# Moving one gate step in the projection phase, and splitting the last norm of a two-layer hybrid decoder trunk

## The chip, the cores and the metric

The kernel runs on one core of one Trainium2 chip. The metric is the device time of one execution in microseconds (us). An execution under the hardware profiler gives the rows shown below; the plain executions give the median.

## What is computed

Two layers, each of two sublayers with a LayerNorm behind each. 256 tokens, model width 1024, everything float32:

```python
for l in range(2):
    proj = x @ w_in[l]            # rnn input, GeLU gate, q / kv latents, rotary key, gates A and B
    y_rnn = gelu(g_rnn) * rg_lru(causal_dwconv(x_rnn), gx_w, ga_w, ...)   # gate_x, gate_a: 16 blocks of 64
    y_mla = mla_attention(q_lat, kv_lat, k_rope, ...)                     # 16 heads, causal
    mix = (sigmoid(gate_a) * y_rnn + sigmoid(gate_b) * y_mla) @ w_out
    x = layer_norm(ALPHA * x + mix, ln1_g, ln1_b)
    ffn = (gelu(conv3(x @ w_up)[gate]) * conv3(x @ w_up)[val]) @ w_down   # d_ff 3072
    x = layer_norm(ALPHA * x + ffn, ln2_g, ln2_b)
```

## The kernel before

**Precision.** Each float32 operand is split into a rounded part (hi) and a rest (lo): ScalarE (ACT) writes hi with a copy, VectorE (DVE) writes lo with a subtraction. A product is then three matmuls, hi·hi, hi·lo and lo·hi (`mm3`, lines 191 to 193). Weights come from HBM by DMAs of the SP queue into four buffers `raw`, and `load_split` (lines 182 and 183) splits each key in two halves of 1024 columns into the tiles `wh` and `wl`, which have six buffers each, so three keys at a time. A buffer comes free when the last matmul that reads it is done.

**Tiling.** Tokens are two tiles of 128 rows (`t` = 0, 1), channels are chunks of 128. `proj_pair` makes one projection of 256 channels for all 256 tokens: 2 halves (m) x 8 chunks x 3 = 48 matmuls of 256 columns into one bank of PSUM, each half of the bank by 24 of them. The first half of the weights is read last by the 36th matmul, the second by the 48th.

**The order.** TensorE (PE) runs in the order in which the program issues; the other engines are put in order by a planner (a list scheduler with its own simulated times) within what the dependences and `behind` allow. For the mixer sublayer the issue order is the string `ORDER`, a list of steps run once per layer. The steps that matter here:

- `x0` to `x3` (`conv_branch`): one projection each, then per chunk of 128 channels a convolution: ACT line 598, three DVE steps on line 601, then the split of the result into `xch` (ACT, line 607) and `xcl` (DVE, line 608).
- `P` with a digit (`fetch`): load and split of one key of the list `FETCH`: `P6` the recurrent gates' weights, `P8` and `P9` and `Pa` the gate-A keys 1, 2 and 3, `Pb`, `Pc`, `Pd` the gate-B keys 0, 1 and 2.
- `e0` to `e3` (`gates`, line 611): for two chunks each, 6 matmuls per chunk on `xch`, `xcl` and the weights of `P6`, then two sigmoids on ACT (line 619) per chunk. `e3` works on chunks 6 and 7, the output of `x3`.
- `a0` to `a3` (`gate_branch`): one projection with a gate-A key, one sigmoid on ACT (line 626), one product on DVE (line 628).
- `N` (`rnn_gates`): DVE and ACT work on all gates, with four long activations of each kind. `act_step` keeps the sigmoids and the activations of `N` in program order on ACT.

In each layer PE therefore runs ... a1, e2, e3, a2, a3, h1 (a gate-B projection) ... and the six buffers of `wh` hold, at that time, the weights of `P6` until `e3` has read them.

**The end.** `finish` (line 357) runs the last accumulation of a down (or output) projection: it completes tile 0, issues the norm of tile 0, then the last five chunks of tile 1 (for `h` = 0, then for `h` = 1, 512 columns and one PSUM bank each, 15 matmuls per `h`), then the norm of tile 1. `LayerNorm.tile` (line 389) does, per half of 512 columns, the residual add out of PSUM (line 397) and the statistics (line 401), then the aggregate (402), 403, the power on GpSimd (404), and for the very last norm lines 408 and 411 for each half and one DMA of 256 KB for each half from the SP queue (line 413).

**The start.** Lines 202 to 206 issue `WARM` = 8 float32 matmuls of zeros (two passes each in the profile) ahead of the first real matmul, while the first transfers arrive.

Of the kernel before, what the change touches and what calls it, by code (L numbers as in the profile page):

```python
# [11 lines left out]
F32 = mybir.dt.float32  # L12
# [3 lines left out]
ALU = mybir.AluOpType  # L16

P = 128
D = 1024
S = 256  # L20
NT = S // P
# [21 lines left out]
ORDER = (  # L43
# [5 lines left out]
)  # L49
HELD = 4  # L50
WARM = 8
KORD = (0, 1, 4, 5, 2, 3, 6, 7)
NPAIR = DFF // P
ALPHA = (2 * DEPTH) ** 0.25
# [69 lines left out]
def trunk(ctx, tc, x_tok, x_chan, pos, wts, par, lnrow, consts, out):  # L124
    nc = tc.nc
    A = nc.scalar
    V = nc.vector
# [6 lines left out]
    sm = ctx.enter_context(tc.tile_pool(name="sm", bufs=2))  # L134
# [5 lines left out]
    def bank(name):  # L140
        return pp.tile([P, 512], F32, tag="pb", name=name)
# [48 lines left out]
    def mm3(o, lh, ll, rh, rl, start, stop):  # L190
        T.matmul(o, lhsT=lh, rhs=rh, start=start, stop=False)  # L191
        T.matmul(o, lhsT=lh, rhs=rl, start=False, stop=False)  # L192
        T.matmul(o, lhsT=ll, rhs=rh, start=False, stop=stop)  # L193
# [10 lines left out]
    spare = bank("spare")  # L204
    for _ in range(WARM):
        T.matmul(spare[:, :P], lhsT=idle, rhs=idle, start=True, stop=True)
# [23 lines left out]
    for i in range(1, 4):  # L230
# [9 lines left out]
        out=mask[:, P:], in_=mask[:, P:], pattern=[[-1, P]],  # L240
# [106 lines left out]
        return hi[:, o + a:o + b], lo[:, o + a:o + b]  # L347

    def out_last(accs, t, n, wts_of, act_of, hc):
        for h, c in hc:  # L350
            hi, lo = wts_of(c)
            ah, al = act_of(c)
            mm3(accs[t][h], ah[:, t * P:(t + 1) * P], al[:, t * P:(t + 1) * P],
                hi[:, 512 * h:512 * h + 512], lo[:, 512 * h:512 * h + 512],
                False, c == n - 1)

    def finish(ln, accs, n, wts_of, act_of, late):
        out_last(accs, 0, n, wts_of, act_of, [(h, n - 1) for h in range(2)])
        ln.tile(0, accs)
        hc = [(h, c) for h in range(2) for c in range(n - late, n)]  # L360
        out_last(accs, 1, n, wts_of, act_of, hc[:-HELD])
        if not ln.last:
            ln.turn(0)
        out_last(accs, 1, n, wts_of, act_of, hc[-HELD:])
        ln.tile(1, accs)
# [9 lines left out]
    class LayerNorm:  # L375
# [13 lines left out]
        def tile(self, t, accs):  # L389
            l, last = self.l, self.last  # L390
            z = big.tile([P, D], F32, tag="xres", name="z", bufs=4)
            st = sm.tile([P, 2, 6], F32, tag="st", name="st")
            mv = sm.tile([P, 2], F32, tag="mv", name="mv")
            rs = sm.tile([P, 1], F32, tag="rs", name="rs")
            hs = [slice(512 * h, 512 * h + 512) for h in range(2)]
            for h in range(2):
                V.scalar_tensor_tensor(
                    out=z[:, hs[h]], in0=self.xres[t][:, hs[h]], scalar=ALPHA, in1=accs[t][h],
                    op0=ALU.mult, op1=ALU.add,
                )  # L400
                V.bn_stats(st[:, h], z[:, hs[h]])
            V.bn_aggr(mv, st.rearrange("p a b -> p (a b)"))
            V.tensor_scalar(out=rs, in0=mv[:, 1:2], scalar1=EPS, scalar2=None, op0=ALU.add)
            G.tensor_tensor(out=rs, in0=rs, in1=nhalf[:, 0:1], op=ALU.pow)
            g, b = self.gb
            if last:
                for h in range(2):
                    V.scalar_tensor_tensor(out=z[:, hs[h]], in0=z[:, hs[h]], scalar=mv[:, 0:1],
                                           in1=g[:, hs[h]], op0=ALU.subtract, op1=ALU.mult)
                for h in range(2):  # L410
                    V.scalar_tensor_tensor(out=z[:, hs[h]], in0=z[:, hs[h]], scalar=rs,
                                           in1=b[:, hs[h]], op0=ALU.mult, op1=ALU.add)
                    nc.sync.dma_start(out=out[t * P:(t + 1) * P, hs[h]], in_=z[:, hs[h]])
                return
            nmr = sm.tile([P, 1], F32, tag="nmr", name="nmr")
            V.scalar_tensor_tensor(out=nmr, in0=mv[:, 0:1], scalar=-1.0, in1=rs,
                                   op0=ALU.mult, op1=ALU.mult)
            for c in (0, 256):
                V.tensor_scalar(out=z[:, c:c + 256], in0=z[:, c:c + 256], scalar1=mv[:, 0:1],
                                scalar2=rs, op0=ALU.subtract, op1=ALU.mult)  # L420
            A.activation(z[:, hs[1]], z[:, hs[1]], AF.Identity, scale=rs, bias=nmr)
            self.res.append(z)
# [85 lines left out]
    for l in range(DEPTH):  # L508
# [335 lines left out]
        later[0] = False  # L844
        ln = LayerNorm(l, 0, xres, False)
        finish(ln, oacc, 8, lambda c: ow[c], mer_of, 5)
        tp = [bank("upt") for _ in range(NB)]

# [84 lines left out]
        for j in range(NPAIR - LAG, NPAIR - 1):  # L933
            out_chunk(dacc, j, dw[j], hq[j], (0, 1) if j < NPAIR - LATE else (0,))
        ln = LayerNorm(l, 1, xres, l == DEPTH - 1)
        finish(ln, dacc, NPAIR, lambda c: dw[c], lambda c: hq[c], LATE)
        if l < DEPTH - 1:
            xs, xres = ln.xs, ln.res
# [119 lines left out]
```

## Time and profile before

| | us |
|---|---|
| median of 3 runs | 804.9 (804.83 to 805.35) |
| the profiled execution, its own time | 804.24 |
| its span, first to last instruction | 802.4 |
| PE busy in the span | 791.0 |
| DVE, ACT busy | 650.5, 509.1 |
| granted TensorE clock, mean | 0.997 |

The profiled execution is 0.66 us below the median. PE is busy nearly all the time, so what remains to be read is where it is not: 802.4 - 791.0 = 11.4 us, of which the last 7.4 us lie behind its last matmul.

### The profile page before, as it was taken

What the parts mean: (1) busy time and instruction counts of PE and PEld (TensorE: products, weight loads), DVE (VectorE), ACT (ScalarE), POOL (GpSimd) and SP (SyncE); (2) the same over time, 40 slices, a digit from 0 to 9 for tenths busy, and PEclk for the clock granted to TensorE, in tenths of its full rate; (3) what the DMA queues carried; (4) which work ended last, traced back from release to release, by engine and by line L of the source; (5) the groups of instructions that cost most, each with busy time, mean ns of one, the idle gap of its engine ahead of it and who ended that gap; (6) DMA issues with size and microseconds to landing.
All of it is one profiled execution on the core that took longest, in us unless ns stands there. A gap on an engine that the chain in (4) does not pass through costs nothing.

```text
span 802.4 us, 14518 instructions
## 1 busy us (share of the span) xinstructions
PE 791.0 (99%) x5712; PEld 741.2 (92%) x5712; DVE 650.5 (81%) x1260; ACT 509.1 (63%) x910; POOL 10.9 (1%) x27
## 2 busy tenths in 40 slices
PE   9999999999999999999999999999999999999996
PEld 8999899878999999999899999998799999999994
DVE  6998889997699977667777886999887998677755
ACT  5765987783777465556475579688567665555540
POOL 1000000000000000000000000000000000000000
PEclk9999999999999999999999999999999999999998
DMA  8955436524356655435625544563524756655311
GB/s 313 344 185 211 152 115 242 187 85 181 158 210 263 210 177 209 174 122 218 236 79 201 183 169 139 173 219 121 208 76 184 276 196 211 210 165 203 106 53 53
DMA packets 26468, 144.76 MB, mean 180 GB/s; under 512 B 3360, under 2 KB 7072, under 8 KB 11808
## 3 DMA queue, kind: packets, MB, share of 16 engines
q1 hardware_dynamic: 26400, 143.84, 50.6%
q8 instruction: 45, 0.74, 0.4%
q14 instruction: 23, 0.19, 0.1%
HBM read 140.68 MB, written 1.05 MB: 177 GB/s over the span
## 4 chain that ended last, share of the span: by engine, by line
PE 97%; DMA 1%; DVE 1%; ACT 1%; SPq 0%; issue 0%; DVEq 0%
PE proj L193 18%; PE proj L191 18%; PE proj L192 18%; PE dacc L191 6%; PE dacc L192 6%; PE dacc L193 6%; PE oacc L191 2%; PE oacc L192 2%; PE oacc L193 2%; PE sps L756 2%; PE yps L797 2%; PE ptp L783 1%; PE latp L192 1%; PE latp L193 1%; PE latp L191 1%; PE sps L754 1%
## 5 line engine op out<-in xcount | busy, mean ns | idle before, releaser
L193 PE MATMUL proj<-xhi,wl 128*128 128x256 f32 x1216 | 344.2, 283 | 0.1
L191 PE MATMUL proj<-xhi,wh 128*128 128x256 f32 x1216 | 344.1, 283 | 0.0
L192 PE MATMUL proj<-xlo,wh 128*128 128x256 f32 x1216 | 343.6, 283 | 0.0
L183 DVE TENSOR_TENSOR wl<-raw,wh 128x1024 fp32r<-128x1024 f32 (+5 forms) x226 | 241.9, 1089 | 50.4 <-ACT wh L182 49.9
L182 ACT ACTIVATE wh<-raw 128x1024 fp32r<-128x1024 f32 (+5 forms) x226 | 208.7, 952 | 103.0 <-PE proj L192 88.4
L192 PEld LDWEIGHTS proj<-xlo,wh 128*128 128x128 f32 x1216 | 232.9, 192 | 1.7
L191 PEld LDWEIGHTS proj<-xhi,wh 128*128 128x128 f32 x1216 | 232.9, 192 | 1.6
L193 PEld LDWEIGHTS proj<-xhi,wl 128*128 128x128 f32 x1216 | 232.9, 192 | 0.7 <-DVE wl L183 0.7
L899 DVE SCALAR_TENSOR_TENSOR u<-proj,par,u 128x255 f32<-128x255 f32 (+1 forms) x176 | 83.5, 479 | 39.2 <-ACT u L896 37.1
L896 ACT ACTIVATE u<-proj,par 128x256 f32<-128x256 f32 x88 | 49.1, 558 | 94.0 <-DVE u L899 71.5
L191 PE MATMUL dacc<-wsh,hh 128*128 128x512 f32 x192 | 76.2, 397 | 0.0
L192 PE MATMUL dacc<-wsl,hh 128*128 128x512 f32 x192 | 75.9, 395 | 0.0
L193 PE MATMUL dacc<-wsh,hl 128*128 128x512 f32 x192 | 75.9, 395 | 0.0
L183 DVE TENSOR_TENSOR wsl<-raw,wsh 128x1024 fp32r<-128x1024 f32 (+2 forms) x66 | 69.8, 1077 | 0.0
L182 ACT ACTIVATE wsh<-raw 128x1024 fp32r<-128x1024 f32 (+2 forms) x66 | 59.7, 937 | 0.0
L193 PEld LDWEIGHTS dacc<-wsh,hl 128*128 128x128 f32 x192 | 36.1, 188 | 8.9
L191 PEld LDWEIGHTS dacc<-wsh,hh 128*128 128x128 f32 x192 | 36.2, 189 | 7.0
L192 PEld LDWEIGHTS dacc<-wsl,hh 128*128 128x128 f32 x192 | 36.1, 188 | 6.9
L196 ACT ACTIVATE hh<-u 128x256 fp32r<-128x256 f32 x48 | 19.6, 408 | 13.7 <-DVE u L907 13.7
L191 PE MATMUL oacc<-wh,mhi 128*128 128x512 f32 x64 | 26.6, 415 | 0.0
L192 PE MATMUL oacc<-wl,mhi 128*128 128x512 f32 x64 | 25.0, 391 | 0.0
L193 PE MATMUL oacc<-wh,mlo 128*128 128x512 f32 x64 | 25.0, 391 | 0.0
(213 smaller groups left out, 1132.2 us busy)
## 6 DMA issues: line engine op xcount, KB each, us to landing
raw<-in_wts SPq DMA_DIRECT2D x114, 1024.0 KB, 4.9
raw<-in_wts SPq DMA_DIRECT2D x8, 832.0 KB, 4.9
gb<-in_lnrow SPq DMA_DIRECT2D x8, 512.0 KB, 8.0
raw<-in_wts SPq DMA_DIRECT2D x4, 672.0 KB, 4.1
raw<-in_wts SPq DMA_DIRECT2D x7, 336.0 KB, 6.6
raw<-in_wts SPq DMA_DIRECT2D x4, 512.0 KB, 4.5
xres<-in_x_tok SPq DMA_DIRECT2D x2, 512.0 KB, 6.0
k<-krot SPq DMA_DIRECT2D x8, 128.0 KB, 2.4
```

Of the source, the lines that this page charges most:

```text
L182: behind(A.activation(h, w, AF.Copy), after[0])
L183: lo_ins = V.tensor_tensor(out=lo[:, c - a:d - a], in0=w, in1=h.bitcast(F32), op=ALU.subtract)
L191: T.matmul(o, lhsT=lh, rhs=rh, start=start, stop=False)
L192: T.matmul(o, lhsT=lh, rhs=rl, start=False, stop=False)
L193: T.matmul(o, lhsT=ll, rhs=rh, start=False, stop=stop)
L196: A.activation(hi, src, AF.Copy)
L754: T.matmul(sps[:, :P], lhsT=q96[:, h4, :P], rhs=k96[:, h4, :P], start=True, stop=True)
L756: T.matmul(sps[:, P:P + S], lhsT=q96[:, h4, P:], rhs=k96[:, h4], start=True, stop=True)
L783: T.transpose(ptp[:, b * P:(b + 1) * P], sns[hh][:, b * P:(b + 1) * P], ident)
L797: T.matmul(yps[hh * 64:hh * 64 + 64, t * P:S], lhsT=vs[:, hv:hv + 64], rhs=pts[hh][:, 2 * t * P:(2 + t) * P], start=t == 0, stop=t == 1)
L896: ea = A.activation(dst, src, AF.Identity, scale=pcol(l, "fw", 96 + ch), bias=pcol(l, "fb", ch))
L899: ev = V.scalar_tensor_tensor(out=dst[:, k:], in0=src[:, :S - k], scalar=pcol(l, "fw", 48 * (2 - k) + ch), in1=dst[:, k:], op0=ALU.mult, o ...
```

## The change

Three edits. In `ORDER` the step `e3` goes behind `a2` and `Pc`, in both layers. `WARM` goes from 8 to 7. In the last norm, the accumulation of tile 1's second half of 512 columns is issued as two parts of 256 columns (all five chunks for the first part, then all for the second), its residual add and statistics are done in four pieces of 256 columns, and the rows of both token tiles are written in three pieces of 512, 256 and 256 columns, the middle one from the ACT queue.

```diff
-    "e3 a2 Pc N a3 h1 R0 Pd h2 h0 b0+ w0 R1 p0 Pe h3 q0 b1+ r0 L1+ b2 k0 v01 p1 r1 s0 q1 "
+    "a2 Pc e3 N a3 h1 R0 Pd h2 h0 b0+ w0 R1 p0 Pe h3 q0 b1+ r0 L1+ b2 k0 v01 p1 r1 s0 q1 "
-WARM = 8
+WARM = 7
@@ out_last
-        for h, c in hc:
-            hi, lo = wts_of(c)
+        for h, c, *cols in hc:
+            a, b = cols or (0, 512)
+            hi, lo = (w[:, 512 * h + a:512 * h + b] for w in wts_of(c))
             ah, al = act_of(c)
-            mm3(accs[t][h], ah[:, t * P:(t + 1) * P], al[:, t * P:(t + 1) * P],
-                hi[:, 512 * h:512 * h + 512], lo[:, 512 * h:512 * h + 512],
-                False, c == n - 1)
+            mm3(accs[t][h][:, a:b], ah[:, t * P:(t + 1) * P], al[:, t * P:(t + 1) * P],
+                hi, lo, False, c == n - 1 and b == 512)
@@ finish
-        hc = [(h, c) for h in range(2) for c in range(n - late, n)]
+        if ln.last:
+            hc = [(h, c, a, a + w) for h, a, w in ((0, 0, 512), (1, 0, 256), (1, 256, 256))
+                  for c in range(n - late, n)]
+        else:
+            hc = [(h, c) for h in range(2) for c in range(n - late, n)]
@@ LayerNorm.tile
-            for h in range(2):
+            w = 256 if last and t == NT - 1 else 512
+            n = D // w
+            for h in range(n):
+                cs = slice(w * h, w * h + w)
+                acc_h = accs[t][w * h // 512][:, w * h % 512:w * h % 512 + w]
                 V.scalar_tensor_tensor(
-                    out=z[:, hs[h]], in0=self.xres[t][:, hs[h]], scalar=ALPHA, in1=accs[t][h],
+                    out=z[:, cs], in0=self.xres[t][:, cs], scalar=ALPHA, in1=acc_h,
                     op0=ALU.mult, op1=ALU.add,
                 )
-                V.bn_stats(st[:, h], z[:, hs[h]])
-            V.bn_aggr(mv, st.rearrange("p a b -> p (a b)"))
+                V.bn_stats(st[:, h], z[:, cs])
+            V.bn_aggr(mv, st[:, :n].rearrange("p a b -> p (a b)"))
@@ LayerNorm.tile, last norm
-                for h in range(2):
-                    V.scalar_tensor_tensor(out=z[:, hs[h]], in0=z[:, hs[h]], scalar=rs,
-                                           in1=b[:, hs[h]], op0=ALU.mult, op1=ALU.add)
-                    nc.sync.dma_start(out=out[t * P:(t + 1) * P, hs[h]], in_=z[:, hs[h]])
+                for i, (c, d) in enumerate(((0, 512), (512, 768), (768, 1024))):
+                    V.scalar_tensor_tensor(out=z[:, c:d], in0=z[:, c:d], scalar=rs,
+                                           in1=b[:, c:d], op0=ALU.mult, op1=ALU.add)
+                    dma = nc.scalar if i == 1 else nc.sync
+                    dma.dma_start(out=out[t * P:(t + 1) * P, c:d], in_=z[:, c:d])
```

## Rows read from the trace of the kernel before

**Rows 1.** Page, part 1: busy us (share of span) and instructions.
```profile
PE 791.0 (99%) x5712; PEld 741.2 (92%) x5712; DVE 650.5 (81%) x1260; ACT 509.1 (63%) x910; POOL 10.9 (1%) x27
```

**Rows 2.** Waits of PE, whole span: waiter, awaited, total us, times, longest.
```profile
PE gates L192 <- DVE xcl L608: 1.0, 1, 1.0
PE gates L191 <- ACT xch L607: 0.8, 1, 0.8
PE latp L191 <- ACT wh L182: 0.6, 2, 0.3
```

**Rows 3.** Timeline of PE, layer 0: start, us, instruction, [idle before <-releaser].
```profile
85.62 0.28 PE L193 MATMUL gates<-xch,wl 128*128 128x256 f32 x1
86.71 0.38 PE L191 MATMUL gates<-xch,wh 128*128 128x256 f32 x1 [0.82 <-ACT xch L607]
88.09 0.38 PE L192 MATMUL gates<-xcl,wh 128*128 128x256 f32 x1 [0.99 <-DVE xcl L608]
...
88.78 0.29 PE L191 MATMUL proj<-xhi,wh 128*128 128x256 f32 x1
```

**Rows 4.** Timeline of ACT, the same stretch.
```profile
85.24 1.12 ACT L182 ACTIVATE wh<-raw 128x1024 fp32r<-128x1024 f32 x1
86.19 0.47 ACT L607 ACTIVATE xch<-xc 128x256 fp32r<-128x256 f32 x1
...
90.06 2.13 ACT L182 ACTIVATE wh<-raw 128x1024 fp32r<-128x1024 f32 x2
...
93.19 1.06 ACT L182 ACTIVATE wh<-raw 128x1024 fp32r<-128x1024 f32 x1 [0.28 <-PE proj L192]
94.62 1.06 ACT L182 ACTIVATE wh<-raw 128x1024 fp32r<-128x1024 f32 x1 [0.38 <-PE proj L192]
```

**Rows 5.** Timeline of DVE, the same stretch.
```profile
87.61 0.42 DVE L608 TENSOR_TENSOR xcl<-xc,xch 128x256 fp32r<-128x256 f32 x1
...
91.27 2.36 DVE L183 TENSOR_TENSOR wl<-raw,wh 128x1024 fp32r<-128x1024 f32 x2 [0.59 <-ACT wh L182]
```

**Rows 6.** Timelines of DVE and PE, the same place in layer 1.
```profile
480.22 0.42 DVE L608 TENSOR_TENSOR xcl<-xc,xch 128x256 fp32r<-128x256 f32 x1
...
481.47 0.28 PE L191 MATMUL gates<-xch,wh 128*128 128x256 f32 x1
```

**Rows 7.** Timeline of all engines, the end.
```profile
794.17 0.39 PE L192 MATMUL dacc<-wsl,hh 128*128 128x512 f32 x1
...
794.40 0.40 PE L193 MATMUL dacc<-wsh,hl 128*128 128x512 f32 x1
794.84 0.69 DVE L397 SCALAR_TENSOR_TENSOR z<-z,dacc 128x512 f32<-128x512 f32 x1 [0.83 <-PE dacc L193]
795.56 0.69 DVE L401 BATCH_NORM_STATS2 st<-z 128x6 f32<-128x512 f32 x1
...
797.92 1.41 DVE L411 SCALAR_TENSOR_TENSOR z<-z,rs,gb 128x512 f32<-128x512 f32 x2
```

**Rows 8.** Timeline of DVE, two independent 256-column steps back to back.
```profile
617.47 0.47 DVE L899 SCALAR_TENSOR_TENSOR u<-proj,par,u 128x255 f32<-128x255 f32 x1
...
617.86 0.47 DVE L899 SCALAR_TENSOR_TENSOR u<-upf,par,u 128x254 f32<-128x254 f32 x1
```

**Rows 9.** Timelines of PE and ACT: a half bank is read after a projection.
```profile
760.64 0.28 PE L193 MATMUL proj<-xhi,wl 128*128 128x256 f32 x1
...
760.96 0.56 ACT L896 ACTIVATE u<-proj,par 128x256 f32<-128x256 f32 x1 [2.32 <-PE proj L193]
```

**Rows 10.** Windows at the end: us, busy by engine, clock, DMA share, GB/s.
```profile
799.60:800.20 0.60, 0.00 (x0) 0.00 (x0) 0.00 (x0) 0.00 (x0) 0.00 (x0) 0.50 1.02 379
800.20:800.60 0.40, 0.00 (x0) 0.00 (x0) 0.00 (x0) 0.00 (x0) 0.00 (x0) 0.50 1.06 394
```

**Rows 11.** Timeline of PE and ACT, the start.
```profile
1.05 3.78 PE L206 MATMUL spare<-idle 128*128 128x128 f32 x16 [1.05 <-DVE lruw L334]
...
9.52 1.76 ACT L182 ACTIVATE wh<-raw 128x336 fp32r<-128x336 f32 x4 [0.23 <-DMA raw<-in_wts]
```

More of the change, by code (lines that the diff above doesn't have):

```diff
@@ L391, in tile @@
             z = big.tile([P, D], F32, tag="xres", name="z", bufs=4)
-            st = sm.tile([P, 2, 6], F32, tag="st", name="st")
+            st = sm.tile([P, 4, 6], F32, tag="st", name="st")
             mv = sm.tile([P, 2], F32, tag="mv", name="mv")
```

## The prediction

> **What bounds the kernel now.** I read the page's table of engines first [rows 1]: PE is busy 791.0 of 802.4 us, so nothing but PE's work, or the time in which PE does not work, can move the end. Of the 11.4 us in which it does not, 7.4 lie behind its last matmul and most of the rest at the start. The second view is the list of PE's waits over the whole span [rows 2]: behind the start (`latp`) there are two, both of the matmuls of one step, on `xch` and on `xcl`, each once. The timeline of PE says where [rows 3]: in layer 0, in `e3`, chunk 7. Chunk 6 issues its last matmul at 85.62, then PE waits for `xch` until 86.71, then for `xcl` until 88.09, and `a2` begins at 88.78. In the time before it, ACT [rows 4] was splitting weights (85.24) ahead of `xch` (86.19), and DVE wrote `xcl` only at 87.61 [rows 5]. In layer 1 the same `xcl` ends at 480.64, 0.8 us ahead of the matmuls of chunk 7 at 481.47 [rows 6]: no stall there. So there is one hole in the middle, and a tail.
>
> **The move of e3.** What the hole costs: matmuls of 256 columns issue every 0.12 us (the releases by the 36th and the 48th matmul of `a2` lie 1.43 us apart, 12 matmuls [rows 4]). Without a wait chunk 7's six matmuls would follow 85.62 and end 7 x 0.12 = 0.84 later, `a2` at 86.46. It began at 88.78: 2.3 us. After the change `a2` issues where `e3` stood, from 85.62 - 5 x 0.12 = 85.0, takes 48 x 0.12 = 5.8 and ends at 90.8. `e3` follows, 12 matmuls, 1.4 us, to 92.2. By 90.8 `xcl` has been there for 2.8 us (written by 88.03 [rows 5]), so the wait is covered even if DVE were 2 us later; that it is ready by then at all rests on ACT and DVE reaching it no later than now, and nothing that is moved stands ahead of it. `a2` itself needs its weights, which were loaded and split before: now it starts at once at 88.78, and the nearest split on ACT before that is 85.24, of a later key. The gain in layer 0 is 2.3 us, in layer 1 nothing, as there is no wait to save.
>
> What the move puts at risk is the buffers. `e3` is the last reader of the recurrent gates' weights, a pair of the six `wh`/`wl` buffers. Now that pair is filled again, both halves back to back, at 90.06, just behind `e3`, and it holds `a3`'s weights (the pairs of a projection come 1.4 us apart, as at 93.19 and 94.62, this one does not [rows 4]). After the change `a2` ends before `e3`, so its two halves come free first. They were refilled 4.4 and 5.8 us after its start [rows 3, 4], so now at 89.4 and 90.9. From there 1.06 for hi on ACT and 1.2 for lo on DVE [rows 4, 5]: ready at 91.7 and 93.2. `a3` starts at 92.2 and needs the second half 12 matmuls later, at 93.6. Both fit with about 0.4 us to spare; now the second lo ends at 93.6 and `a3` starts 5.8 us behind 88.78, 0.9 later [rows 3, 5]; the next keys have a whole projection more. In layer 1 the intervals are the same and so is the margin. What is queued there: on ACT `a2`'s sigmoid could go between the two splits, about 0.5 us, which would use up the second margin and cost 0 to 0.2. The gates' four sigmoids of `e3` come 1.4 us after `a2`'s end, ahead of `N`, which then starts in step with PE. On SP `Pc`'s one DMA goes ahead of `e3`, which issues none, and no queue of GpSimd is touched. I take 0, bounds 0 to +0.5 for the two layers. PE has no other wait behind this place [rows 2], so I let the 2.3 us arrive at the end.
>
> **The tail.** Today the last matmul issues at 794.40; the residual add starts at 794.84 and the statistics at 795.56 [rows 7]. The idea on paper is that two pieces of 256 columns leave less to do behind the last matmul: one add and one statistics of about 0.42 rather than two of 0.69, 0.5 us less. That holds only if DVE may read the first half of the bank while PE still fills the second. The trace has this case in every up-projection, whose half m = 0 is complete 24 matmuls before the end: ACT stood idle for 2.32 us and began the read of that half at 760.96, behind the projection's last matmul at 760.64 (0.28 long) [rows 9]. So a half bank was not read before the bank was finished, and I expect the same here: all of the second 512 columns waits for the last matmul as now. The Trainium skill, "PSUM — Partial Sum Buffer", section "PSUM bank collisions raise a hardware error", tells why a program is built so: it asks to guard PSUM by bank and not by address, since two engines in one bank at disjoint columns collide. By that rule the split gains nothing; by column, it would gain the 0.5.
>
> Without the overlap: 15 matmuls of 512 columns at 0.23 (794.17 to 794.40 [rows 7]) become 30 of 256 at 0.12, 3.5 to 3.6 us: +0.1; the last one is 0.12 shorter but issues 0.11 later. DVE behind it: two steps, 1.4 us, become four. At a cadence of 0.39 [rows 8] and 0.45 for the last that is 1.6; at half a 512-column step each it is 1.4. I take +0.1, bounds 0 to +0.2. The pieces of the first 512 columns and tile 0's extra step are hidden: DVE idles 0.83 us before the last add [rows 7], and the additions there are three steps' fixed cost of about 0.1 each. Line 411 becomes three steps, 1.5 for 1.41, but its last DMA is not what sets the end alone: the 16 DMA engines are filled from 799.6 to 800.6 by the first piece and the last [rows 10], the first piece is as large as before, and the bytes are the same. So three pieces and a second issuing queue buy nothing that the engines have to give, and cost little: 0, bounds -0.2 (a smaller last piece lands sooner) to +0.2 (one more step, shorter rows). No DMA of the ACT queue stands in this trace; its first one, in tile 0, lies beside PE's last matmuls. Tail: +0.2, bounds -0.1 to +0.5.
>
> **The warming matmul.** The 16 passes run from 1.05 to 4.83, 0.2 us each [rows 11]; one matmul less ends 0.4 us earlier, about when the first real weights arrive. The start ends on transfers, not on PE: at 9.52 ACT still waits for a transfer of weights [rows 11] and PE waits with it, 0.6 us in two places [rows 2]. So the time saved is lost there: 0. The Trainium skill, "TensorE: Matmul & The Clock Gate", "Part 1: The HAM clock gate", says that the slow clock is the default and that sustained activity lifts it, so that a gap in the warming could keep PE slow for longer. The gap here would be at most the 0.4 us taken away, and PE's two waits for transfers would take up most of what a slower clock costs: 0 to +0.3, an estimate.
>
> **Sum.** -2.3 + 0 + 0.2 + 0 = -2.1. On the profiled execution 804.24 gives 802.1; that execution is 0.7 under the median, so the median goes from 804.9 to 802.8, 0.26% less. A measurement of this kernel can tell about 0.2% (1.6 us) from no change.
>
> **The rivals.**
> - *The split works by column*: DVE reads the first half of the bank early. For it: nothing in the arithmetic forbids it. Against it: [rows 9]. -2.3 - 0.5 + 0.2 = -2.6, or 802.2. Chance 0.10.
> - *The hole moves on by half*: the planner puts the sigmoids or another split ahead of `a3`'s second half, or later in `N`, and PE waits for some 0.6 us in each layer. For it: the margin falls to 0.4 us, and ACT is what delayed `xch`. Against it: PE waits nowhere else. About -0.9, 804.0. Chance 0.14.
> - *a3 waits for e3's buffers*, the slower side. If the planner gives `a3` the pair that `e3` reads, as now, rather than `a2`'s, its split starts at 92.4, the first lo is ready at 92.4 + 1.0 + 1.2 = 94.6 against a need at 92.2: 2.4 us in each layer. In layer 0 that eats the gain, in layer 1 it comes on top: +2.4 + 0.2, 807.5. It decides by which buffer is free first: `a2`'s first half would be, by 2.8 us. Chance 0.07.
> - *The edit of the order doesn't do what it says*: `xcl` slips behind `a2`'s work and `e3` waits still; some 804.9. Chance 0.03.
>
> **How the numbers follow.** The forecast, 802.8, with its own range 802.2 to 803.4, has 0.66. Faster by over 0.2% means below 803.3: 0.61 of that, and 0.10 of the split, 0.71. Slower: 0.07, and 0.01 of the third. Same: the rest, 0.21. The range leaves out the slow case, the fourth and the outer ends: 801.9 to 804.3.
>
> **What would show it.** In the profile after: no wait on `xch` or `xcl` in PE's list, in layer 0 `a2`'s matmuls follow `e2`'s without a gap and `a3` begins 7.2 us after `a2`'s start; the pair of splits behind `a2` 1.4 us apart and released by a projection; in the tail the first add on columns 512 to 767 begins only behind the last matmul, and the last transfer lands within 0.3 us of where it did against the last matmul. I am wrong if PE waits for `wh` or `wl` at `a3`, if that add starts early, or if the hole shows up again further on.

## The result, and the profile after

The changed kernel takes 809.28 us (median of 5 runs, 807.96 to 810.99) where the kernel before, beside it, takes 804.90 (804.73 to 805.71): a ratio of 1.0054, 95% interval 1.0034 to 1.0074. It is slower; the forecast was 802.8, faster, and the range ended at 804.3.

PE is busy as long as before to 0.3 us, in a longer span (page, part 1, against [rows 1]):

```profile
PE 791.3 (98%) x5725; PEld 742.8 (92%) x5725; DVE 651.5 (81%) x1266; ACT 508.2 (63%) x910; POOL 10.2 (1%) x27
```

The hole is gone, and others have opened. The list of PE's waits over the whole span of the changed kernel, which answers to [rows 2] (waiter, awaited, total us, times, longest):

```profile
PE proj L193 <- DVE wl L183: 5.7, 3, 2.5
PE latp L191 <- ACT wh L182: 1.2, 1, 1.2
```

No wait on `xch` or `xcl` is left. A projection now waits three times for the lo half of its weights. PE's timeline tells where. The first two rows answer to [rows 3]: in layer 0 `e3` follows the last matmul of `a2` without a pause. Then `h3` (the gate-B projection of key 3, fetched by `Pe`) in layer 0 and in layer 1, and last the first projection at the start:

```profile
91.38 0.28 PE L193 MATMUL proj<-xhi,wl 128*128 128x256 f32 x1
91.50 0.28 PE L191 MATMUL gates<-xch,wh 128*128 128x256 f32 x1
...
117.16 0.28 PE L192 MATMUL proj<-xlo,wh 128*128 128x256 f32 x1
119.90 0.39 PE L193 MATMUL proj<-xhi,wl 128*128 128x256 f32 x1 [2.46 <-DVE wl L183]
...
514.46 0.28 PE L192 MATMUL proj<-xlo,wh 128*128 128x256 f32 x1
517.21 0.38 PE L193 MATMUL proj<-xhi,wl 128*128 128x256 f32 x1 [2.47 <-DVE wl L183]
...
21.68 0.28 PE L192 MATMUL proj<-xlo,wh 128*128 128x256 f32 x1
22.72 0.39 PE L193 MATMUL proj<-xhi,wl 128*128 128x256 f32 x1 [0.76 <-DVE wl L183]
```

The same place in the kernel before was not among the rows shown, because the list of PE's waits has nothing for it. It should have been read: the third matmul of `h3` follows the second by 0.33 us instead of 0.12, that is, PE was already 0.2 us early.

```profile
118.78 0.28 PE L192 MATMUL proj<-xlo,wh 128*128 128x256 f32 x1
119.11 0.39 PE L193 MATMUL proj<-xhi,wl 128*128 128x256 f32 x1
```

What DVE does ahead of those lo halves in the changed kernel, layer 0 (L670 is the scan of the recurrence, L668 the product ahead of it; the last row's first instruction is the one that `h3` waits for):

```profile
111.39 2.28 DVE L670 TENSOR_TENSOR_SCAN th<-ga,gx 128x1024 f32<-128x1024 f32 x1
113.59 1.20 DVE L668 TENSOR_TENSOR gx<-gx,th 128x1024 f32<-128x1024 f32 x1
114.71 0.68 DVE L637 TENSOR_TENSOR gl<-gl,sg 128x512 f32<-128x512 f32 x1
115.32 1.22 DVE L183 TENSOR_TENSOR wl<-raw,wh 128x1024 fp32r<-128x1024 f32 x1
116.45 2.28 DVE L670 TENSOR_TENSOR_SCAN th<-ga,gx 128x1024 f32<-128x1024 f32 x1
118.65 3.20 DVE L183 TENSOR_TENSOR wl<-raw,wh 128x1024 fp32r<-128x1024 f32 x3
```

And the granted clock: in two stretches behind that wait, the changed kernel's windows (us, busy time and instructions of PE, PEld, DVE, ACT, POOL, then the granted clock, DMA share, GB/s):

```profile
120.40:123.70 3.30, 3.30 (x18) 3.30 (x17) 3.27 (x8) 0.00 (x0) 0.00 (x0) 0.50 0.48 164
124.00:130.00 6.00, 6.00 (x52) 6.00 (x51) 4.43 (x6) 3.70 (x7) 0.00 (x0) 1.00 0.48 113
```

Behind the wait of layer 0 the clock is granted at 0.50 (1.2 of 2.4 GHz) for some 3.4 us, in which a matmul of 256 columns issues every 0.21 us instead of 0.12. Ahead of the wait (115 to 117 us), and behind the equal wait of layer 1, it is 1.00.

The difference of the two spans, 807.5 - 802.4 = 5.1 us, adds up from the starts of the same matmuls in both timelines:

```
part of the span                                   after minus before
start, up to the first turn of the latents         +0.7   (the 1.04 us gap at 21.68 is 0.9 too long)
layer 0, to the first scores                       +1.6   = -2.2 hole, +2.4 wait at h3, +1.5 clock, -0.1 other
layer 1, to the first scores                       +2.4   = the wait at h3 (2.75 now, 0.33 before)
the end                                            +0.4
```

The 1.5 for the clock is the distance from `h3`'s third matmul to the first scores, 13.16 us in layer 0 and 11.67 in layer 1, where no such stretch is.

### The profile page after: what moved, and what is told of

Same layout as the page of the kernel before. It is cut to its first block, busy times and chain, and to the rows that moved or that the text cites. A ratio compares the mean times of both kernels' runs of the same rounds, so it can differ in the third digit from the quotient of the medians.

```text
span 807.5 us, 14552 instructions
## 1 busy us (share of the span) xinstructions
PE 791.3 (98%) x5725; PEld 742.8 (92%) x5725; DVE 651.5 (81%) x1266; ACT 508.2 (63%) x910; POOL 10.2 (1%) x27
## 4 chain that ended last, share of the span: by engine, by line
PE 92%; ACT 4%; issue 1%; DVE 1%; DMA 1%; SPq 0%; DVEq 0%; ACTq 0%
PE proj L193 17%; PE proj L191 17%; PE proj L192 17%; PE dacc L191 6%; PE dacc L192 6%; PE dacc L193 6%; PE oacc L191 2%; PE oacc L192 2%; PE oacc L193 2%; PE sps L765 2%; PE yps L806 2%; ACT wh L182 1%; PE ptp L792 1%; PE latp L192 1%; PE latp L193 1%
## 5 line engine op out<-in xcount | busy, mean ns | idle before, releaser
L191 PE MATMUL dacc<-wsh,hh 128*128 128x512 f32 (+1 forms) x197 | 77.0, 391 | 0.0
L192 PE MATMUL dacc<-wsl,hh 128*128 128x512 f32 (+1 forms) x197 | 76.8, 390 | 0.0
L193 PE MATMUL dacc<-wsh,hl 128*128 128x512 f32 (+1 forms) x197 | 76.7, 390 | 0.0
```

## The experiments

**The three parts apart.** Four kernels were run beside the kernel before (its 30 executions: 804.2 us median). The move alone:

```
-    "e3 a2 Pc N a3 h1 R0 Pd h2 ...
+    "a2 Pc e3 N a3 h1 R0 Pd h2 ...
```

> The move of e3 alone, in both layers; start and tail as before. Theory A (the later e3 delays N, so that on DVE the second recurrence scan falls ahead of the lo split of h3's weights, and PE waits there): PE's wait on xch and xcl in layer 0 is gone (-2.3 us), PE waits about 2.5 us for wl at the projection h3 in both layers (+5 us), so about +2.7 us, 807.6, and up to 3.4 us more in executions in which the granted clock falls behind these waits. Theory B (the loss comes from the start or the tail, the move itself gains as forecast): 802.6, and no wait at h3.

Measured: 807.26 us, ratio 1.0036 (1.0022 to 1.0050). Its profile has the two waits at `h3`, and none on the x splits:

```profile
PE proj L193 <- DVE wl L183: 4.9, 2, 2.5
```

The last norm alone (out_last, finish and LayerNorm.tile as in the change):

```
+        if ln.last:
+            hc = [(h, c, a, a + w) for h, a, w in ((0, 0, 512), (1, 0, 256), (1, 256, 256)) ...
+                for i, (c, d) in enumerate(((0, 512), (512, 768), (768, 1024))):
```

> The last norm alone: accumulation in two parts, four pieces of statistics, three pieces of rows; e3 and WARM as before. If a half bank is read only behind the bank's last matmul: the add of columns 512 to 767 starts behind the last matmul, +0.2 to +0.5 us, 805.3. If it could be read early: that add starts about 3 us earlier and the time falls by 0.3 to 0.5 us, 804.5.

Measured: 805.59 us, ratio 1.0012 (1.0003 to 1.0021). In its profile the time behind the last matmul's slot (0.23 us for 512 columns, 0.12 for 256) to the end of the span is 8.06 us, where it was 7.76: 0.3. The rest of its 1.0 us need not be the tail's: in the profiled execution the granted clock fell to 0.50 at 89.17 us, behind the old hole of `e3`, and that alone took 1.5 us (from `e3`'s last matmul to `h3`'s third 31.94 us, where it is 30.44 without).

One warming matmul less, alone:

```
-WARM = 8
+WARM = 7
```

> One warming matmul less alone. If it only takes work off PE while transfers arrive: 0, 804.9. If the 0.7 us by which the changed kernel is behind at 34 us come from it (the planner orders DVE differently in the first 50 us, and PE waits for wl near 22 us): +0.7, 805.6, with that wait in PE's list. If they come from transfers that landed later in that one execution: 0 on the median, with no wait for wl.

Measured: 805.14 us, ratio 1.0007 (0.9998 to 1.0016), which by itself doesn't tell it from no change. But the profile has a new wait at the start, the one seen in the changed kernel, and the first turn of the latents starts at 34.47 us, where it lay between 32.0 and 33.6 in every profile with eight matmuls:

```profile
PE proj L193 <- DVE wl L183: 0.8, 1, 0.8
```

The planner orders ACT and DVE by the times it expects. One matmul less on PE gave it another order, and ACT's rows show the step that matters, first in the kernel before, then here (L484 reads the latents out of PSUM):

```profile
18.99 2.01 ACT L182 ACTIVATE wh<-raw 128x1024 fp32r<-128x1024 f32 x2 [1.38 <-DVE lruw L337]
20.90 0.92 ACT L484 ACTIVATE lat<-latp 128x336 f32<-128x336 f32 x2
```
```profile
20.38 0.45 ACT L484 ACTIVATE lat<-latp 128x336 f32<-128x336 f32 x1 [2.88 <-PE latp L193]
20.73 2.00 ACT L182 ACTIVATE wh<-raw 128x1024 fp32r<-128x1024 f32 x2
```

The two hi copies came first; now they stand behind a read that waits 2.88 us for PE, and the lo split that follows them is late. In the changed kernel the order is the same (the read at 20.01, the copies at 20.35).

The move in layer 0 alone:

```
+        order = ORDER if l else ORDER.replace("e3 a2 Pc N", "a2 Pc e3 N")
```

> The move of e3 in layer 0 alone. Theory A (N is delayed by the move itself, in each layer for itself): -2.3 for the hole, +2.6 for the wait at h3 in layer 0, no wait at h3 in layer 1: 805.2, up to 1.7 more where the clock falls behind the wait. If the wait at h3 came only from PE being ahead of a chain that has not moved, layer 0 would show the same here, and layer 1 of the changed kernel (where PE is not ahead) no wait: its 2.5 us there speak against that.

Measured: 803.98 us, ratio 1.0000 (0.9990 to 1.0009), with one wait left, at `h3` of layer 0. So in layer 0 the new wait gives back what the hole took, and in layer 1, which had no hole, it is a plain loss: all of the 0.36% of the move.

```profile
PE proj L193 <- DVE wl L183: 2.5, 1, 2.5
```

The product, 1.0036 x 1.0012 x 1.0007 = 1.0055, agrees with the change's 1.0054 within the intervals.

**Is it the scan ahead of the splits?** The second scan was put behind `h3`'s lo splits on DVE, and its step `R1` behind the fetch `Pe`, on top of the move:

```
+    "a2 Pc e3 N a3 h1 R0 Pd h2 h0 b0+ w0 p0 Pe R1 h3 ...
+            behind(V.tensor_tensor_scan(...), last_split[0] if i else None)
```

> The move of e3 in both layers as in the change, and one thing more: the second scan of the recurrence is held on VectorE behind the lo halves of h3's weights (and stands behind the fetch of those weights in the written order). The tail and the warming matmuls are those of the kernel before. Theory: TensorE's 2.46 us waits at h3 come from the 2.28 us scan that stands ahead of h3's lo splits on VectorE. Then both waits fall from 2.5 us each to under 0.5 us, the removed hole at e3 stays removed, and the program is 1.5 to 2.5 us faster than the kernel before (ratio 0.997 to 0.998), or 4 to 6 us faster than the move alone (which was 1.0036). Rival: the splits are late because their own hi copies on ScalarE are late behind the later tanh, exp and sqrt chain; then the waits at h3 stay above 1.5 us and the ratio above 1.002. In between: the scan only explains its share, waits of 0.5 to 1.5 us, ratio 0.998 to 1.001; or the wait goes to whoever needs the second scan's result (the attention and output steps behind it), which would show as a new wait of about 2 us further on.

Measured: 813.12 us, ratio 1.0102 (1.0086 to 1.0117).

```profile
PE oacc L191 <- DVE k L729: 4.2, 2, 2.1
PE sps L754 <- issue: 2.2, 2, 1.1
...
PE proj L193 <- DVE wl L183: 0.6, 2, 0.3
```

At `h3` the theory holds: the waits fall from 2.5 to 0.3. The time gets worse all the same: in both layers a wait of 1.1 us stands among the scores and one of 2.1 us in the output projection, and behind the latter the clock fell to 0.50 (at 167.0 and 566.4). That wait is put down to a copy of `k` that DVE made at 165.49, behind three splits (163.57); the planner had reordered DVE there as well. Why it put those splits first was not tried. What the run shows is that the scan, with the product ahead of it, was the last link, and that DVE has no room for it a little later: from 115 to 120 us it is busy for all 5.00 us in the windows of this kernel, as in those of the kernel before.

**The head of the chain.** The order of the kernel before, and the hole filled from its other side: x3's last hi and lo split ahead of `e0`'s sigmoids and of gate-B key 0's split, in layer 0 alone.

```
+            first = tuple(last_xch) if l == 0 and key == ("gb", 0) else ends
+            held[key] = load_split(l, key, ((0, 1024), (1024, 2048)), after=first)
...
+                if l == 0 and c == 0:
+                    act_step(last_xch[0])
```

> The order of steps as in the kernel before; instead, in layer 0 alone, the hi and lo split of x3's last column block (the one that e3 waits for) is put ahead of e0's sigmoids on ScalarE and ahead of the split of the first gate-B weights. So the hole at e3 is filled from its other side, and no gate step and no sigmoid comes later. Theory: the change lost because e3's sigmoids, and the tanh, exp and sqrt chain behind them, came later while TensorE came earlier to h3; here both come 2.3 us earlier together. Then TensorE's waits on the x splits (1.0, 0.8) are mostly gone, the wait at h3 stays under 0.7 us, and the program is about 2.0 us faster than the kernel before (ratio 0.9970 to 0.9985). Rival: h3 waits whenever TensorE reaches it earlier, since h3's splits are paced by ScalarE and VectorE on their own; then a wait of 1.5 to 2.5 us stands at h3 in layer 0 and the ratio is 0.999 to 1.001.

Measured: 802.63 us (802.25 to 803.23) beside 805.05, ratio 0.9974 (0.9964 to 0.9984): faster than both kernels.

```profile
PE gates L191 <- ACT ga L624: 0.8, 1, 0.8
PE proj L193 <- DVE wl L183: 0.4, 1, 0.4
```

The wait at `h3` is 0.4, though PE comes there 1.2 us earlier than before, since `e3` and all that follows from it come earlier too. The waits on the x splits are gone, but 0.8 us of the hole stays under another name (a bank of the gates that an earlier step's sigmoids, now later on ACT, release late). In the profile the first scores come 0.9 us nearer to the first turn of the latents, not 2.0; where the rest of the measured gain (2.1 us by the ratio) came from is told below with the clock.

**The chain's length.** Two runs went at it directly. In the first, the move with the hi copies of `h2`'s weights held behind the second tanh:

```
+            late = nend if key == ("gb", 2) else ends
```

> The move of e3 in both layers as in the change, and one thing more: the hi copies of h2's weights (the gate-B weights, key 2) are held on ScalarE behind the second tanh, where the move alone let them slip between the two tanhs (in that run tanh at 94.87 and 98.25 us, with two copies at 95.85 and 97.29 between, and the first exp at 100.59; in the kernel before the first exp stood at 99.38). Tail and warming as before. Theory: the wait at h3 is the length of the chain from e3's sigmoids over tanh, exp, sqrt and the two scans to h3's lo splits; TensorE reaches h3 2.3 us earlier, the chain doesn't. Taking the two copies out of the chain makes it 1 to 2 us shorter, so the waits at h3 fall from 2.5 us to between 0.3 and 1.3 us in each layer and the ratio from 1.0036 to between 0.997 and 1.0005. Rival: the chain's pace is set elsewhere (VectorE, the release of buffers); then the waits at h3 stay over 2 us and the ratio at 1.002 to 1.005.

Measured: 819.24 us, ratio 1.0176 (1.0162 to 1.0189); the waits at `h3` grew to 3.0 us. The expectation missed. More than half of the loss lies further on: like the kernel with the moved scan it waits 2.1 us in the output projection of each layer, it waits 1.4 among the values, and the clock fell to 0.50 twice (at 120.6 and 571.1). ACT's timelines show why the waits at `h3` grew. First the changed kernel's two copies, which stand between its tanhs at 96.34 and 99.72; then this kernel (L644 is tanh, L655 the roots):

```profile
97.32 1.06 ACT L182 ACTIVATE wh<-raw 128x1024 fp32r<-128x1024 f32 x1
98.76 1.06 ACT L182 ACTIVATE wh<-raw 128x1024 fp32r<-128x1024 f32 x1 [0.38 <-PE proj L192]
```
```profile
97.19 1.06 ACT L644 ACTIVATE th<-ga 128x1024 f32<-128x1024 f32 x1 [1.21 <-DVE ga L640]
...
100.53 1.99 ACT L182 ACTIVATE wh<-raw 128x1024 fp32r<-128x1024 f32 x2
...
104.32 1.67 ACT L182 ACTIVATE wh<-raw 128x768 fp32r<-128x768 f32 x2
...
108.25 2.01 ACT L655 ACTIVATE th<-th 128x1024 f32<-128x1024 f32 x2
```

The copies did leave the tanhs, and ACT then stood idle for 1.21 us. They came back between the exps, and two copies of the next key, of which one had stood between the roots, now came ahead of them: the roots ended at 110.26, where they ended at 109.53 with the move alone. So the pace seems to be ACT's whole work in this stretch, not one pair of copies (no run here took work off ACT); holding one pair back only changed what it delays.

In the second, the kernel before with each tanh done twice, which writes the same values again:

```
                 act_step(A.activation(th, ga[i], AF.Tanh))
+                act_step(A.activation(th, ga[i], AF.Tanh))
```

> The kernel before, with each tanh done twice, one right behind the other (the second writes the same values again): two more ScalarE instructions of 1.0 us in the chain in each layer, and nothing moved on TensorE. Theory: the chain from e3's sigmoids to h3's lo splits is what h3 waits for, and in the kernel before it ends just as TensorE arrives (0.2 us of wait). Two microseconds more in the chain then stand as a wait of 1.5 to 2.5 us at h3 in each layer, 3 to 5 us in all, and a fall of the granted clock behind some of them: ratio 1.004 to 1.008. Rival: h3 waits in the changed kernel only because TensorE comes early, and the chain has room of 2 us in the kernel before; then h3 waits under 0.7 us in both layers and the ratio is 0.9995 to 1.0015.

Measured: 809.90 us, ratio 1.0062 (1.0050 to 1.0075), with the hole of `e3` as before and, in both layers, 1.9 us at `h3` (the third of the three is 0.4 us at the start):

```profile
PE proj L193 <- DVE wl L183: 4.3, 3, 1.9
PE gates L192 <- DVE xcl L608: 1.0, 1, 1.0
```

Nothing moved on PE here, and 2 us more in the chain came out as 2 us of wait. So the chain from the tanhs on had no room in the kernel before. Taken together, in the timelines of all these kernels, layers 0 and 1 (PE: the time that PE's own matmuls take from the last one of `e3` to the third of `h3`; chain: the time that it took; us):

```
kernel                       PE            chain
before                  30.24  30.24   30.44  30.44
change                  24.48  24.48   27.11  27.11
the move alone          24.48  24.48   27.11  27.11
the move in layer 0     24.48  30.24   27.11  30.44
scan behind h3's lo     24.48  24.48   24.92  24.93
x split first           30.24  30.24   30.81  30.44
each tanh twice         30.23  30.24   32.32  32.33
```

This is the mechanism in numbers. Between `e3`'s last matmul and the lo half that `h3` needs lie four sigmoids, two tanhs, four exps and two roots on ACT (not four of each kind) and two products and two scans on DVE. In the kernel before this takes as long as PE's work in that stretch, to 0.2 us, in both layers. But there it does not run on from `e3`: on ACT the first tanh stands behind `a2`'s sigmoid (`sg`) and behind two weight copies that `a2`'s matmuls release. ACT in layer 0 of the kernel before, then of the changed kernel, then of the one with the last norm alone:

```profile
95.59 0.58 ACT L626 ACTIVATE sg<-proj 128x512 f32<-128x512 f32 x1
96.07 2.00 ACT L641 ACTIVATE th<-ga 128x1024 f32<-128x1024 f32 x2
```
```profile
93.73 2.02 ACT L182 ACTIVATE wh<-raw 128x1024 fp32r<-128x1024 f32 x2
95.63 0.48 ACT L628 ACTIVATE gx<-gates,par 128x256 f32<-128x256 f32 x1
95.98 0.49 ACT L628 ACTIVATE ga<-gates,par 128x256 f32<-128x256 f32 x1
96.34 1.08 ACT L650 ACTIVATE th<-ga 128x1024 f32<-128x1024 f32 x1
```
```profile
94.65 1.06 ACT L182 ACTIVATE wh<-raw 128x1024 fp32r<-128x1024 f32 x1 [1.78 <-PE proj L192]
97.53 2.00 ACT L650 ACTIVATE th<-ga 128x1024 f32<-128x1024 f32 x2
```

The move takes `a2`'s 48 matmuls, 5.76 us, out of PE's stretch. The first tanh, which came 7.41 us behind `e3`'s last matmul (88.66), now comes 3.54 behind it (92.80), 3.9 less, as `a2` no longer comes between; from the first tanh to `h3` it takes 23.56 where it took 23.04, 0.5 more, with two copies between the tanhs. So the chain loses 3.3, and the missing 2.4 are the wait. The third kernel confirms that the chain before hung on `a2`: there `a2` ran in part at the half clock, the first tanh came 1.5 us later (8.90 behind `e3`'s last matmul at 88.63), and `h3` still waited only 0.2. One rival stays untested: the first tanh reads chunks 0 to 3 alone and none of `e3`'s results, and only ACT's fixed order puts it behind `e3`'s sigmoids and the two copies (93.73) among them. No run changed that order, so whether the move could gain with another one is open.

**Does DVE wait for the bank?** The last norm as in the change, with the last five chunks of columns 768 to 1023 accumulated in a bank of their own and joined by one more addition:

```
+            own = bank("dlast")
+                mm3(own[:, :256], ah[:, P:2 * P], al[:, P:2 * P], hi, lo, c == n - late, c == n - 1)
+                if h == 3:
+                    V.tensor_tensor(out=z[:, cs], in0=z[:, cs], in1=own[:, :256], op=ALU.add)
```

> The last norm alone as in the change (columns 512 to 1023 of the last tile in two parts, three pieces written), with one difference: the last five chunks of columns 768 to 1023 are accumulated in a PSUM bank of their own, and one more VectorE addition of 128x256 joins them. Theory: in the change the two additions of the second half both began behind the last matmul because VectorE reads no part of a bank that TensorE still accumulates in; with a bank of its own the add and the statistics of columns 512 to 767 run before the last matmul, the time from the last matmul to the end falls by about 0.5 to 0.7 us against the last norm alone, and the program comes out at 0.9993 to 1.0002 of the kernel before, where the last norm alone had 1.0012. Rival: the wait is not the bank's (VectorE is held by its own earlier work or by the order of the program); then the additions of columns 512 to 767 still start behind the last matmul, the extra addition costs 0.35 us, and the ratio is 1.001 to 1.002.

Measured: 804.91 us, ratio 0.9997 (0.9988 to 1.0006). First the end of the changed kernel (PE's last matmul, then DVE), then that of this one (the last matmul into the old bank, DVE, the last matmul of all, DVE):

```profile
799.26 0.28 PE L193 MATMUL dacc<-wsh,hl 128*128 128x256 f32 x1
799.58 0.75 DVE L405 SCALAR_TENSOR_TENSOR z<-z,dacc 128x256 f32<-128x256 f32 x2 [0.61 <-PE dacc L193]
800.25 0.74 DVE L409 BATCH_NORM_STATS2 st<-z 128x6 f32<-128x256 f32 x2
```
```profile
792.69 0.28 PE L193 MATMUL dacc<-wsh,hl 128*128 128x256 f32 x1
...
793.76 0.73 DVE L413 SCALAR_TENSOR_TENSOR z<-z,dacc 128x256 f32<-128x256 f32 x2
...
794.46 0.28 PE L193 MATMUL dlast<-wsh,hl 128*128 128x256 f32 x1
795.07 0.40 DVE L418 TENSOR_TENSOR z<-z,dlast 128x256 f32<-128x256 f32 x1
```

With the last quarter of the columns in its own bank, both additions from the old bank begin before the last matmul (793.76 against 794.46); in the changed kernel they begin behind it. So what held DVE is a guard on the bank, or on the tile that fills it, which this run can't tell apart, and not DVE's own work. The gain in the trace is less than expected: behind the last matmul's slot 7.82 us, where it was 8.06 with the last norm alone and 7.76 in the kernel before. DVE, with more and smaller steps, only comes to the last addition 0.5 us behind that slot. The Trainium skill, "PSUM — Partial Sum Buffer", section "PSUM bank collisions raise a hardware error", asks to guard by bank; the two orders above agree with it.

The x split first, and this norm, in one kernel:

> The x split of layer 0 put ahead of e0's sigmoids (order of steps as in the kernel before) and the last norm with a bank of its own, together, with eight warming matmuls. Theory: the two edits touch separate places and add: about -2.0 us from the hole and 0 to -0.4 us at the end against the kernel before, ratio 0.9965 to 0.9985. Rival (a wait at h3 takes the hole's place): 0.999 to 1.001, as for the x split alone.

Measured: 802.95 us, ratio 0.9981 (0.9971 to 0.9990). The bank of its own adds nothing to the x split alone (0.9974); the intervals overlap.

## Why the prediction was wrong

**The step that failed** is the last of the part on `e3`: that `N` "then starts in step with PE", that "PE has no other wait behind this place", and so that the 2.3 us arrive at the end. A wait list with nothing in it was read as room. It says only that whoever comes second comes no more than a little second: the two instructions on either side of `h3`'s pause in the kernel before, 118.78 and 119.11, already had PE 0.2 us ahead of DVE. And what the move needs there is not room for the 2.3 us by which PE comes earlier but for the 5.76 by which `e3` comes nearer to `h3`: moving a producer behind another step shortens the distance to its consumer by the whole length of that step. Of these 5.76 the chain gave back 3.3. In the prediction's own terms: the first tanh of `N` had come 1.65 us behind the last matmul of the pair `e3`, `a2` (94.42 to 96.07) and came 3.54 behind it (92.80 to 96.34), as `e3`'s sigmoids and two copies now stand between; these 1.9 us and the 0.5 behind it are the 2.4 of the wait. The prediction worked the distance out for `a3`'s buffers and not for `e3`'s own results, and for the same reason took layer 1 to be free, where the move cost 2.4 us.

**The rivals.** "The hole moves on by half" had the right place in general terms (later, in `N`, in each layer) and a quarter of the right size (0.6 us in each layer, where it was 2.4). "`a3` waits for `e3`'s buffers" was the right sign for a wrong cause: `a3` waits for nothing. That its 2.4 us in each layer, 807.5 in all, come close to what the move alone took (807.26) is luck. (The rival on the split by column comes to 802.3 by its own sum, not 802.2.)

**Right in mechanism and size.** The hole went: `a2` starts at 85.74 behind `e2`'s last matmul, `e3` follows at 91.50 without a wait, and `a3` at 92.92 comes 7.18 us behind `a2`'s start (7.2 forecast). `a3`'s two hi copies lie 1.44 us apart and are released by a projection, as forecast, in place of the pair back to back of [rows 4]:

```profile
90.14 1.08 ACT L182 ACTIVATE wh<-raw 128x1024 fp32r<-128x1024 f32 x1
91.58 1.06 ACT L182 ACTIVATE wh<-raw 128x1024 fp32r<-128x1024 f32 x1 [0.36 <-PE proj L192]
```

**The tail** was right in its main point and within its bounds: the additions of columns 512 to 767 wait for the last matmul, as [rows 9] had it. The time behind the last matmul grew by 0.3 to 0.4 us, but not where the forecast put it. The additions and statistics there take 1.41 us from first to last in both kernels (0.1 more forecast); the aggregate takes 0.05 more, the three last steps 0.13 more, and the rest is the writing of the rows; for these 0 was taken. That the size comes near is in part luck. (Behind the last matmul of the kernel before lie 802.4 - 794.80 = 7.6 us, not 7.4; no argument hangs on it.)

**The warming matmul** was taken as 0 to +0.3 and cost 0.7 us in the changed kernel's profile, 1.1 alone. The two mechanisms weighed (transfers, clock) are not it. It went through the planner: the wait at 21.68 us stands for a lo split whose hi copy ACT, in its new order, made only behind a read that waits for PE. That an edit of PE's timing reorders ACT and DVE elsewhere was priced for the sigmoids only.

**Left out** altogether: that a wait may cost more than its length. The hole was priced at 2.3; with the clock behind it, it seems to have cost the kernel before some 1.4 us more in about half of its executions (below).

## What to carry to other kernels

An empty list of waits is no measure of slack: before moving a step, follow its own results to the next instruction on the bounding engine that needs them, and compare the length of that chain with the distance that is left. Here a hole in front of a step was better closed by making its input earlier (1.3 to 2.1 us gained) than by moving the step later (nothing gained by the move in that layer), since the first brings the step and its consumers forward together, and the second leaves less of PE's work to cover the chain behind it. Where a planner lays out the other engines, price every edit with a trace of the whole program, as even one instruction less at the start can shift a copy.

## What the runs showed of the hardware

A wait of about 1.9 to 3.0 us, or two of 0.8 and 1.0 together, in otherwise unbroken matmul work can be followed by 3.4 us at half the granted clock, which costs 1.5 us more, and it isn't always: in the twelve profiles it followed 8 of 18 such places. It followed the wait at `h3` in layer 0 of the changed kernel and not the equal one in layer 1; the hole of `e3` in the kernel with the new last norm and not in that of the kernel before. The six profiles with such a stretch have a mean granted clock of 0.994 or 0.995 over the span, the six without one 0.997 or 0.998 (none lies at 0.996). So the mean clock of the executions that were not profiled sorts them into two groups:

```
                        mean clock 0.997 or more     0.996 or less
kernel                  runs   us                    runs   us
before, first four      16     803.1 to 804.2        14     804.7 to 805.4
the move alone           3     806.0 to 806.2         4     807.3 to 809.4
the last norm alone      0                           11     803.3 to 806.2
WARM 7 alone             9     804.6 to 805.4         2     806.0 to 806.2
the move in layer 0      6     803.6 to 804.0         4     804.4 to 805.4
before, next four        9     803.4 to 804.6        14     804.8 to 805.9
x split first            8     802.3 to 803.2         0
own bank                 5     803.8 to 804.5         6     804.9 to 805.9
x split and own bank     9     802.6 to 803.4         1     803.7
```

Read by columns, the sums of the traces come out: in the left one the move costs 2.4 us (the waits say 2.6), the move in layer 0 0.2 (0.2), the warming matmul 1.4 (0.7 to 1.1). The x split gains 1.3 there (its span 1.2, of which 0.4 lie at the start, which differs from profile to profile), and the remaining 0.8 of its median comes in because none of its eight executions is in the right column, where the kernel before has 14 of 23: its longest wait behind the start is 0.8 us. That the right column of the kernel before is the clock behind `e3`'s hole is argued from its size, from the profile of the last norm alone, which has the stretch there, and from the x split, where both are gone; the one profile of the kernel before is from the left column and has no such stretch. What decides in one execution whether the clock falls, and why the kernel with the new last norm, the same but for its end, has none of its eleven in the left column, stays open; its cost is therefore taken from the trace and not from its median.
